# A diffusion-transformer layer on one core: attention's state scaling and query scaling in wide vector-engine operations, its output norm on the scalar engine, and a reordered gelu branch

## The chip, the cores and the metric

The kernel runs on one core of a Trainium2 chip. A core has a matrix engine (PE), a vector engine (DVE), a scalar engine (ACT), a general engine (POOL), and queues for DMA transfers, SP's among them. Each engine works through its own list of instructions in order, and waits where an instruction needs something that another engine or a transfer has not delivered. The metric is the device time of one execution in microseconds.

## The reference

One layer with 1024 latent tokens of width 1024 and 256 context tokens. What matters here, cut from the reference:

```
hl = modulate(rmsnorm(x, g_pre_mix), sh1, sc1)            # adaLN; sh1, sc1, gt1 ... from c @ w_ada
z_q, z_k, z_v, z_dec, z_og, z_f, z_rx, z_rg = split(hl @ w_in)
# group 1: bidirectional chunked gated linear attention, 4 heads, dk 64, dv 128
b    = cumsum(log_a);  q_t = q * exp(b);  k_t = k * exp(-b);  k_end = k * exp(b_last - b)
attn = where(tril, q_t @ k_t^T, 0)
o    = attn @ v + q_t @ s                  # s: the state before the chunk
s    = s * exp(b_last) + k_end^T @ v       # starts from the context's final state
y_gla = rmsnorm(o) * g_gla * silu(z_og)
# group 2: 2-D Fourier mixing of z_f.  group 3: centred conv + bidirectional RG-LRU scan h_rg
y_rg = h_rg * gelu(z_rg)
x = x + gt1 * rmsnorm(concat(y_gla, y_f, y_rg) @ w_out, g_post_mix)
x = x + gt2 * rmsnorm(swiglu(modulate(rmsnorm(x, g_pre_ffn), sh2, sc2)), g_post_ffn)
```

## The kernel before

Everything stays in fp32 precision: a product of large matrices is three PE passes (`mm3`, lines 84 to 86: high by high, high by low, low by high part). In names, `z` and `zn` are the banks of PSUM that take the input projection, transposed (`z`, 128x512) or not (`zn`, 128x256), `hl` is the modulated input, `w_hi` and `w_lo` are split weights. `z_v1` is a projection of values (a run of `zn`), `z_rg` the projection that gelu is applied to.

Attention takes two head pairs, p = 0 and 1, with two heads h and two directions d each, and goes over 8 blocks n of 128 tokens. Before the first block the states are made for all blocks (`gla_states`, which calls `gla_kv` for each direction and half q): PE transposes the keys (`k_tr`), multiplies them with the values (`kv`), DVE runs the recurrence (`tt`, line 532, one 128x128 step per block and direction), and ACT writes each state, multiplied by its chunk's exponential, into the state tile `St` (line 518, one 64x128 instruction for each head). The context's keys and states (`ctx_tr`, `ctx_st`) come ahead of that. In `gla_block` each block first forms `qx` = q times exp(c) (four 64x128 products, the two of d = 0 on DVE, those of d = 1 on POOL from the exchanged copy `qTs` of q), then `attn` (four matmuls), the masked `am` (DVE), and the output bank `o` (four matmuls, from `qx` with `St` and from `am` with the values). ACT squares and sums `o` (`jk`, line 587), POOL raises to the power of minus one half (`ors`), and DVE scales `o` into `on` (line 592).

The rest that the text names: `gate_ps` are banks of the RG-LRU gates, which ACT reads; `rg_scan` ends with `hR`, to which the second direction is added (line 648); `fourier` folds its input (`zo`, `zfold`) before the products `Z_ps`; `ada_row` (line 651) makes a row of the modulation: eight `ada_acc` steps of 128x1024 on DVE (line 658), then for each half a matmul that sums over partitions (`row_ps`, line 669) and a DVE step that writes `ada_row` (line 677). PSUM is two rings of four banks: `mm` (z, zn, o, and others) and `aux` (ctx_tr, k_tr, kv, attn, gate_ps, row_ps, Z_ps and others); a bank is free again when its last reader is done.

What order the instructions have on each engine is not written down: the kernel is built in a mode in which a scheduler decides it from the dependencies and its own estimates. Only table functions of ACT are chained in the order of the program. So an edit in one place can move instructions in many.

Of the kernel before, what the change touches and what calls it, by code (L numbers as in the profile page):

```python
# [16 lines left out]
P = 128  # L17
# [21 lines left out]
def tile_trunk(ctx: ExitStack, tc: tile.TileContext, A: dict):  # L39
# [26 lines left out]
    def aux(name="aux"):  # L66
        return psum.tile([P, 512], F32, tag="aux", bufs=4, name=name)
# [291 lines left out]
    def z_v1(blocks, c=False):  # L359
        z_N(w_v[1], 256, lambda ps, m: S.copy(vNc[1] if c else vN[1][m // 4][:, m % 4:m % 4 + 2, :], ps), blocks, c)  # L360
# [151 lines left out]
        return kn, last  # L512

    def gla_kv(p, d, q, kn, gs, tprev):
        def state(m, t):
            n = (7 - m) if d else m
            for h in range(2):
                S.mul(St[p][h ^ d][R[h], n, :], t[R[h]], gs[R[h], m:m + 1])  # L518

        if q == 0:  # L520
            state(0, s_ctx[p][d])
            tprev = s_ctx[p][d]
        kv = aux("kv")
# [12 lines left out]

    def gla_states(p):
# [25 lines left out]
    load(imask, A["imask"])  # L563
    on = [[None] * 2 for _ in range(2)]

    def gla_block(p, n):
        cs = slice(n * P, (n + 1) * P)
        qx, am = hp((P, 2, P), name="qx"), hp((P, 2, P), name="am")
        for d in range(2):
            for h in range(2):  # L570
                (G if d else V).tensor_mul(qx[R[h], h ^ d, :], (qTs if d else qT)[p][R[h], cs], Ex[p][d][R[h], cs])
# [237 lines left out]
    def fourier(zf, blk):  # L809
# [16 lines left out]
        jk = hp(name="fjk")[:, 0:256]
        V.tensor_mul(jk, f[:, 0, :], alt)
# [644 lines left out]
```

## Time and profile before

| | before |
|---|---|
| time, median of 3 runs | 1141.46 us (1141.27 to 1141.75) |
| time of the profiled execution | 1140.04 us |
| its span, first to last instruction | 1138.3 us |
| PE busy | 1082.4 us (95%) |
| DVE, ACT, POOL busy | 807.9 (71%), 506.8 (45%), 107.4 us (9%) |
| mean granted clock of PE | 0.975 |

The span is the length of the trace; the time of the same execution is 1.7 us more. PE is busy for all but 56 us of it. A clock of 1.0 is the full 2.4 GHz, 0.5 is 1.2 GHz; at the lower one the same matmul takes twice as long and PE counts as busy all the while, so a stretch at half clock costs time that no idle figure shows.

### The profile page before, as it was taken

The numbers are of one execution on the slowest core, as the hardware profiler recorded it, in microseconds if no ns is written. First come the engines' busy times: TensorE is split into PE (matmuls) and PEld (weight loads), VectorE is DVE, ScalarE is ACT, GpSimd is POOL, SyncE is SP. The second block draws the span as 40 slices with busy tenths as digits, with TensorE's granted clock in tenths as the row PEclk, the third lists the DMA queues.
The fourth block names the chain that finished last, engine by engine and source line by source line (L and its number), as shares of the span: only waits on it lengthen the run. The fifth ranks groups of instructions, "written<-read, shape, count | busy, mean of one in ns | idle before, by whom it ended". The sixth has DMA issues, their size and how long they took to land.

```text
span 1138.3 us, 15164 instructions
## 1 busy us (share of the span) xinstructions
PE 1082.4 (95%) x5547; PEld 903.2 (79%) x5547; DVE 807.9 (71%) x1386; ACT 506.8 (45%) x964; POOL 107.4 (9%) x133
## 2 busy tenths in 40 slices
PE   4899989989999999949999999999999999999997
PEld 2799887867789888837878888888888888888886
DVE  3474693648878366797879777777777568967684
ACT  3452768486273355654313333232323137654251
POOL 2310001213220011370000000000000000000100
PEclk8899999999999999978999999999999999999999
DMA  9802312112526222351273242324232468867571
GB/s 331 301 20 78 107 38 56 38 39 63 201 75 238 77 93 93 112 166 56 93 253 108 93 130 93 102 93 130 93 102 93 149 208 310 277 221 235 177 283 74
DMA packets 119970, 156.42 MB, mean 137 GB/s; under 512 B 8276, under 2 KB 70996, under 8 KB 119896
## 3 DMA queue, kind: packets, MB, share of 16 engines
q1 hardware_dynamic: 106536, 128.72, 34.7%
q10 hardware_dynamic: 13360, 26.75, 7.0%
q8 instruction: 43, 0.70, 0.2%
q14 instruction: 31, 0.25, 0.1%
HBM read 124.50 MB, written 28.57 MB: 134 GB/s over the span
## 4 chain that ended last, share of the span: by engine, by line
PE 81%; DVE 8%; ACT 4%; DMA 4%; issue 3%; POOL 0%; SPq 0%; DVEq 0%; POOLq 0%; ACTq 0%
PE prod L84 11%; PE prod L85 11%; PE prod L86 11%; PE dn L84 6%; PE dn L86 6%; PE dn L85 6%; PE z L84 3%; PE o_ps L86 3%; PE o_ps L84 3%; PE o_ps L85 3%; PE z L85 3%; PE z L86 3%; DMA wraw<-in_w_in 2%; ACT St L518 2%; PE zn L84 2%
## 5 line engine op out<-in xcount | busy, mean ns | idle before, releaser
L85 PE MATMUL dn<-dr,dl 128*128 128x512 f32 (+1 forms) x319 | 121.8, 382 | 0.0
L86 PE MATMUL dn<-dr,dl 128*128 128x512 f32 (+1 forms) x319 | 121.8, 382 | 0.0
L84 PE MATMUL dn<-dr,dl 128*128 128x512 f32 (+1 forms) x319 | 118.7, 382 | 0.0
L85 PE MATMUL zn<-w_lo,hl 128*128 128x256 f32 (+1 forms) x256 | 74.0, 290 | 0.0
L84 PE MATMUL zn<-w_hi,hl 128*128 128x256 f32 (+1 forms) x256 | 73.4, 289 | 0.2 <-ACT yfr L77 0.2
L86 PE MATMUL zn<-w_hi,hl 128*128 128x256 f32 (+1 forms) x256 | 73.0, 288 | 0.0
L84 PE MATMUL prod<-a,b_hi 128*128 128x512 f32 x176 | 69.6, 395 | 1.4 <-ACT b_hi L91 1.4
L86 PEld LDWEIGHTS dn<-dr,dl 128*128 128x128 f32 x319 | 60.0, 188 | 11.7
L85 PEld LDWEIGHTS dn<-dr,dl 128*128 128x128 f32 x319 | 60.0, 188 | 11.7
L85 PE MATMUL prod<-a,b_hi 128*128 128x512 f32 x176 | 69.2, 393 | 0.0
L84 PEld LDWEIGHTS dn<-dr,dl 128*128 128x128 f32 x319 | 60.0, 188 | 11.5
L84 PE MATMUL prod<-s,wb_hi 128*128 128x512 f32 x176 | 68.9, 391 | 0.0
L85 PE MATMUL prod<-s,wb_hi 128*128 128x512 f32 x176 | 68.5, 389 | 0.0
L86 PE MATMUL prod<-s,wb_lo 128*128 128x512 f32 x176 | 68.3, 389 | 0.0
L86 PE MATMUL prod<-a,b_lo 128*128 128x512 f32 x176 | 68.1, 391 | 0.0
L1110 ACT CAST b<-wf_raw 128x512 fp32r<-128x512 f32 x22 | 13.7, 622 | 115.0 <-PE prod L86 105.4
L84 PE MATMUL z<-hl,w_hi 128*128 128x512 f32 x160 | 64.8, 405 | 0.0
L85 PE MATMUL z<-hl,w_hi 128*128 128x512 f32 x160 | 63.7, 398 | 0.0
L86 PE MATMUL z<-hl,w_lo 128*128 128x512 f32 x160 | 63.4, 396 | 0.0
L1177 ACT CAST dl<-h 128x512 fp32r<-128x512 f32 x77 | 47.7, 620 | 35.0 <-issue 20.6
L1178 DVE TENSOR_TENSOR dl<-h,dl 128x512 fp32r<-128x512 f32 x77 | 52.6, 684 | 12.8 <-ACT dl L1177 12.8
L1234 POOL TENSOR_TENSOR rs<-s,mhalf 128x1 f32<-128x1 f32 x7 | 5.4, 774 | 553.3 <-DVE s L1233 553.3
(362 smaller groups left out, 2871.6 us busy)
## 6 DMA issues: line engine op xcount, KB each, us to landing
ada_raw<-in_w_ada SPq DMA_DIRECT2D x48, 512.0 KB, 6.3
h<-hd SPq DMA_DIRECT2D x77, 256.0 KB, 4.8
wd_raw<-in_w_down SPq DMA_DIRECT2D x77, 256.0 KB, 4.6
hd<-c ACTq DMA_DIRECT2D x55, 256.0 KB, 2.1
wf_raw<-in_w_gate SPq DMA_DIRECT2D x25, 512.0 KB, 4.1
wf_raw<-in_w_up SPq DMA_DIRECT2D x22, 512.0 KB, 4.7
wraw<-in_w_in SPq DMA_DIRECT2D x16, 512.0 KB, 4.2
xb<-in_x SPq DMA_DIRECT2D x8, 512.0 KB, 8.4
```

Of the source, the lines that this page charges most:

```text
L84: PE.matmul(out, lh, rh, start=start, stop=False)
L85: PE.matmul(out, lh, rl, start=False, stop=False)
L86: return PE.matmul(out, ll, rh, start=False, stop=stop)
L518: S.mul(St[p][h ^ d][R[h], n, :], t[R[h]], gs[R[h], m:m + 1])
L1110: S.copy(hi, u[:, 4:8])
L1177: S.copy(t[:, 0, :], raw)
L1178: V.tensor_sub(t[:, 1, :], raw, t[:, 0, :].bitcast(F32))
L1234: G.tensor_tensor(out=r, in0=s1, in1=mhalf, op=ALU.pow)
```

## The change

Five edits. States: the 64 ACT instructions that write `St` become wide DVE products, one for each head, direction and half (64x512 or 64x384), issued after all the `tt` of that half. Queries: `gla_q` forms q times exp(c) for four blocks at once with four 64x512 products on DVE, in place in `qT` and in the tile of exp(c), `la`; POOL has no part in it any more. Output norm: `on` moves from DVE to ACT. POOL's add for `hR` and three folds in `fourier` move to DVE. In the order of the program, all of `z_v1` now stands ahead of the context's states, and `z_rg(1)` right after `z_rg(0)`.

```
--- before.py
+++ after.py
@@ -512,14 +512,15 @@
         return kn, last
 
     def gla_kv(p, d, q, kn, gs, tprev):
-        def state(m, t):
-            n = (7 - m) if d else m
+        def states(m, w, t):
+
+            n = slice(8 - m - w, 8 - m) if d else slice(m, m + w)
             for h in range(2):
-                S.mul(St[p][h ^ d][R[h], n, :], t[R[h]], gs[R[h], m:m + 1])
+                V.tensor_mul(fl(St[p][h ^ d][R[h], n, :], d), t[R[h]], gs[R[h], m:m + w].unsqueeze(2).to_broadcast([64, w, P]))
 
         if q == 0:
-            state(0, s_ctx[p][d])
             tprev = s_ctx[p][d]
+            states(0, 1, tprev.unsqueeze(1))
         kv = aux("kv")
         for i, m in enumerate(order(q)):
             n = (7 - m) if d else m
@@ -530,8 +531,9 @@
         for i, m in enumerate(order(q)):
             tt = t4[:, i, :]
             V.scalar_tensor_tensor(tt, tprev, gs[:, m:m + 1], kv[:, i * P:(i + 1) * P], op0=ALU.mult, op1=ALU.add)
-            state(m + 1, tt)
             tprev = tt
+        w = len(order(q))
+        states(4 * q + 1, w, t4[:, 0:w, :])
         return tprev
 
     def gla_states(p):
@@ -563,23 +565,34 @@
     load(imask, A["imask"])
     on = [[None] * 2 for _ in range(2)]
 
+    qx = [None] * 2
+
+    def gla_q(p, h):
+
+        hs = slice(h * 512, (h + 1) * 512)
+        q, qs, e0, e1 = qT[p], qTs[p], Ex[p][0], Ex[p][1]
+        V.tensor_mul(q[R[0], hs], q[R[0], hs], e0[R[0], hs])
+        V.tensor_mul(e0[R[1], hs], q[R[1], hs], e0[R[1], hs])
+        V.tensor_mul(q[R[1], hs], qs[R[1], hs], e1[R[1], hs])
+        V.tensor_mul(e0[R[0], hs], qs[R[0], hs], e1[R[0], hs])
+        qx[p] = q, e0
+
     def gla_block(p, n):
         cs = slice(n * P, (n + 1) * P)
-        qx, am = hp((P, 2, P), name="qx"), hp((P, 2, P), name="am")
-        for d in range(2):
-            for h in range(2):
-                (G if d else V).tensor_mul(qx[R[h], h ^ d, :], (qTs if d else qT)[p][R[h], cs], Ex[p][d][R[h], cs])
+        if n % 4 == 0:
+            gla_q(p, n // 4)
+        am = hp((P, 2, P), name="am")
         at = [aux("attn")[:, 0:256].rearrange("p (d i) -> p d i", d=2) for _ in range(2)]
         for d in range(2):
             for h in range(2):
-                mark = PE.matmul(at[h][:, d, :], Kt[p][d][R[h], cs], qx[R[h], h ^ d, :], start=True, stop=True)
+                mark = PE.matmul(at[h][:, d, :], Kt[p][d][R[h], cs], qx[p][h ^ d][R[h], cs], start=True, stop=True)
         for h in range(2):
             V.tensor_mul(am[:, h, :], at[h][:, 0, :], wmask)
             V.copy_predicated(am[:, h, :], imask, at[1 - h][:, 1, :])
         o = mm("o")
         for h in range(2):
             oc = o[:, h * P:(h + 1) * P]
-            PE.matmul(oc, qx[:, h, :], St[p][h][:, n, :], start=True, stop=False)
+            PE.matmul(oc, qx[p][h][:, cs], St[p][h][:, n, :], start=True, stop=False)
             PE.matmul(oc, am[:, h, :], vN[p][n // 4][:, n % 4, h * P:(h + 1) * P], start=False, stop=True)
         ss = sm("oss", 2)
         jk = pool.tile([P, P], mybir.dt.bfloat16, tag="jk", bufs=1, name="jk")
@@ -589,7 +602,7 @@
         if n % 4 == 0:
             on[p][n // 4] = pg((P, 4, 256), name="on")
         for h in range(2):
-            V.tensor_scalar_mul(on[p][n // 4][:, n % 4, h * P:(h + 1) * P], o[:, h * P:(h + 1) * P], r[:, h:h + 1])
+            S.mul(on[p][n // 4][:, n % 4, h * P:(h + 1) * P], o[:, h * P:(h + 1) * P], r[:, h:h + 1])
         return mark
 
     def rg_gate(dst, u, blk, d, g, n):
@@ -645,7 +658,7 @@
         if d == 0:
             hR.append(a)
         else:
-            G.tensor_add(hR[blk], hR[blk], a)
+            V.tensor_add(hR[blk], hR[blk], a)
 
 
     def ada_row(c0, fn):
@@ -717,11 +730,10 @@
         vN[1][i] = pg((P, 4, 256), name="vN")
     w_q = [w_T(C_Q)]
     bs = [ctx_exp(p, d) for p, d in PD]
-    z_v1(range(4))
+    z_v1(range(8))
     kws = [ctx_tr(b) for b in bs]
     for (p, d), kw in zip(PD, kws):
         ctx_state(p, d, kw)
-    z_v1(range(4, 8))
     kt_begin(0)
     w_q.append(w_T(C_Q + P))
     def z_steps(w, h, ev):
@@ -814,14 +826,14 @@
         G.memset(o[:, 0:1], 0.0)
         rv = zf[:, 513:1024][:, ::-1]
         V.tensor_add(e[:, 1:512], zf[:, 1:512], rv)
-        G.tensor_sub(o[:, 1:512], zf[:, 1:512], rv)
+        V.tensor_sub(o[:, 1:512], zf[:, 1:512], rv)
         f = pg((P, 4, 256), name="zfold")
         er, orv = e[:, 257:513][:, ::-1], o[:, 257:512][:, ::-1]
         V.tensor_add(f[:, 0, :], e[:, 0:256], er)
         V.tensor_sub(f[:, 1, :], e[:, 0:256], er)
         G.memset(f[:, 2:4, 0:1], 0.0)
-        G.tensor_sub(f[:, 2, 1:], o[:, 1:256], orv)
-        G.tensor_add(f[:, 3, 1:], o[:, 1:256], orv)
+        V.tensor_sub(f[:, 2, 1:], o[:, 1:256], orv)
+        V.tensor_add(f[:, 3, 1:], o[:, 1:256], orv)
         cols = sm("fcol", 3)
         jk = hp(name="fjk")[:, 0:256]
         V.tensor_mul(jk, f[:, 0, :], alt)
@@ -865,11 +877,11 @@
         V.tensor_copy(yfr[2][:, blk, 0:1], cc[:, 0:1])
 
     z_rg(0)
+    z_rg(1)
     ada_step(9)
     w_og = [w_N([(C_OG, 256)])]
     for d in range(2):
         rg_scan(1, d, rg_gates(1, d))
-    z_rg(1)
     ada_step(0)
     alt = hp(name="alt")[:, 0:256]
     load(alt, A["alt"])
```

Where the scheduler put things. On DVE, at the states of p = 0 (names as above; `rgc` belongs to the context's RG-LRU), before:

```order
L532 SCALAR_TENSOR_TENSOR tt_1828<-tt_1828,gs_1753,kv_1819 128x128
L532 SCALAR_TENSOR_TENSOR tt_1848<-tt_1848,gs_1739,kv_1841 128x128
L532 SCALAR_TENSOR_TENSOR tt_1828<-tt_1828,gs_1753,kv_1819 128x128
L532 SCALAR_TENSOR_TENSOR tt_1848<-tt_1848,gs_1739,kv_1841 128x128
L532 SCALAR_TENSOR_TENSOR tt_1865<-tt_1828,gs_1753,kv_1858 128x128
L571 TENSOR_TENSOR qx_1991<-qT_1875,la_709 64x128 x2
L532 SCALAR_TENSOR_TENSOR tt_1865<-tt_1865,gs_1753,kv_1858 128x128 x2
L577 TENSOR_TENSOR am_1992<-attn_1997,cm_65 128x128
L571 TENSOR_TENSOR qx_2036<-qT_1875,la_709 64x128 x2
L578 COPY_PREDICATED am_1992<-imask_714,attn_1998 128x128
L577 TENSOR_TENSOR am_1992<-attn_1998,cm_65 128x128
L578 COPY_PREDICATED am_1992<-imask_714,attn_1997 128x128
```

and after the change, the end of the same piece of work:

```order
L575 TENSOR_TENSOR la_709<-qT_1855,la_709 64x512
L533 SCALAR_TENSOR_TENSOR tt_1849<-tt_1849,gs_1753,kv_1842 128x128
L590 TENSOR_TENSOR am_1975<-attn_1976,cm_65 128x128
L590 TENSOR_TENSOR am_2015<-attn_2016,cm_65 128x128
L574 TENSOR_TENSOR qT_1855<-qT_1855,la_709 64x512
L533 SCALAR_TENSOR_TENSOR tt_1849<-tt_1849,gs_1753,kv_1842 128x128
L576 TENSOR_TENSOR qT_1855<-qTs_1856,la_710 64x512
L591 COPY_PREDICATED am_1975<-imask_714,attn_1977 128x128
L590 TENSOR_TENSOR am_1975<-attn_1977,cm_65 128x128
L577 TENSOR_TENSOR la_709<-qTs_1856,la_710 64x512
L638 SCALAR_TENSOR_TENSOR rgc_1916<-rgc_1916,cx_507 128x512
L519 TENSOR_TENSOR St_1766<-tt_1849,gs_1753 64x3x128
```

In the kernel before nothing but `tt` and two `qx` stands ahead of the first `am`. After the change the last two `St` (one of them is the last row shown, its twin the next row), which `o` of block 0 reads because direction 1 ends at block 0, stand behind two `tt`, the second `gla_q`, four steps of `am` for blocks 0 and 1, and an `rgc`. In the whole piece, from the first `tt` to the last `St`, there are 14 `tt`, 8 wide `St` and the 4 products of the second `gla_q`.

On DVE again, at the rows of the modulation (`ada_row_2920` in the kernel before and `ada_row_2870` after are the row of g_post_mix, `ada_row_2958` and `ada_row_2908` that of g_pre_ffn), before:

```order
L807 TENSOR_TENSOR yfr_2864<-yfr_2864,a_2524 128x256
L807 TENSOR_TENSOR yfr_2865<-yfr_2865,a_2524 128x256
L658 SCALAR_TENSOR_TENSOR ada_acc_2931<-ada_raw_2934,s32_73,ada_acc_2931 128x1024
L658 SCALAR_TENSOR_TENSOR ada_acc_2931<-ada_raw_2937,s32_73,ada_acc_2931 128x1024
L658 SCALAR_TENSOR_TENSOR ada_acc_2931<-ada_raw_2940,s32_73,ada_acc_2931 128x1024
L658 SCALAR_TENSOR_TENSOR ada_acc_2931<-ada_raw_2943,s32_73,ada_acc_2931 128x1024
L658 SCALAR_TENSOR_TENSOR ada_acc_2931<-ada_raw_2946,s32_73,ada_acc_2931 128x1024
L658 SCALAR_TENSOR_TENSOR ada_acc_2931<-ada_raw_2949,s32_73,ada_acc_2931 128x1024
L658 SCALAR_TENSOR_TENSOR ada_acc_2931<-ada_raw_2952,s32_73,ada_acc_2931 128x1024
L658 SCALAR_TENSOR_TENSOR ada_acc_2931<-ada_raw_2955,s32_73,ada_acc_2931 128x1024
L677 SCALAR_TENSOR_TENSOR ada_row_2958<-row_ps_2959,g_row_2961 128x512
```

and after the change:

```order
L819 TENSOR_TENSOR yfr_2760<-yfr_2760,a_2452 128x256
L819 TENSOR_TENSOR yfr_2761<-yfr_2761,a_2452 128x256
L671 SCALAR_TENSOR_TENSOR ada_acc_2881<-ada_raw_2884,s32_73,ada_acc_2881 128x1024
L671 SCALAR_TENSOR_TENSOR ada_acc_2881<-ada_raw_2887,s32_73,ada_acc_2881 128x1024
L671 SCALAR_TENSOR_TENSOR ada_acc_2881<-ada_raw_2890,s32_73,ada_acc_2881 128x1024
L671 SCALAR_TENSOR_TENSOR ada_acc_2881<-ada_raw_2893,s32_73,ada_acc_2881 128x1024
L671 SCALAR_TENSOR_TENSOR ada_acc_2881<-ada_raw_2896,s32_73,ada_acc_2881 128x1024
L690 SCALAR_TENSOR_TENSOR ada_row_2870<-row_ps_2876,g_row_2878 128x512
L671 SCALAR_TENSOR_TENSOR ada_acc_2881<-ada_raw_2899,s32_73,ada_acc_2881 128x1024
L671 SCALAR_TENSOR_TENSOR ada_acc_2881<-ada_raw_2902,s32_73,ada_acc_2881 128x1024
L671 SCALAR_TENSOR_TENSOR ada_acc_2881<-ada_raw_2905,s32_73,ada_acc_2881 128x1024
L690 SCALAR_TENSOR_TENSOR ada_row_2908<-row_ps_2909,g_row_2911 128x512
```

Before, both halves of the first row were written ahead of the eight `ada_acc` of the second. Now the second half, from `row_ps_2876`, stands between the fifth and the sixth of them. On PE, where these banks are filled, the end of the last `z` of the gelu projection before:

```order
L86 MATMUL z_3059<-hl01_494,w_lo_2859 128x512
L84 MATMUL z_3059<-hl01_494,w_hi_2858 128x512
L85 MATMUL z_3059<-hl11_502,w_hi_2858 128x512
L86 MATMUL z_3059<-hl01_494,w_lo_2859 128x512
L669 MATMUL row_ps_2959<-ada_acc_2931,cm_65 128x512
L669 MATMUL row_ps_2964<-ada_acc_2931,cm_65 128x512
L600 MATMUL gate_ps_2990<-uT_707,gates_1905 128x512
L600 MATMUL gate_ps_2993<-uT_707,gates_1905 128x512
```

and after the change:

```order
L86 MATMUL z_2843<-hl01_494,w_lo_2755 128x512
L84 MATMUL z_2843<-hl01_494,w_hi_2754 128x512
L85 MATMUL z_2843<-hl11_502,w_hi_2754 128x512
L86 MATMUL z_2843<-hl01_494,w_lo_2755 128x512
L682 MATMUL row_ps_2876<-ada_acc_910,cm_65 128x512
L682 MATMUL row_ps_2909<-ada_acc_2881,cm_65 128x512
L682 MATMUL row_ps_2914<-ada_acc_2881,cm_65 128x512
L613 MATMUL gate_ps_2940<-uT_707,gates_1885 128x512
```

The matmul for `row_ps_2876` had its counterpart (`row_ps_2926`) 100 rows earlier, between matmuls of `o`. It now stands directly ahead of `row_ps_2909`, which needs the finished `ada_acc`.

## Rows read from the trace of the kernel before

**Rows 1.** Waits of PE: engine, line, waited for: total us, times, longest us.
```profile
PE o L582 <- ACT St L518: 4.4, 1, 4.4
...
PE ctx_tr L449 <- DVE b_c L443: 2.9, 2, 2.6
...
PE gate_ps L600 <- ACT qT L559: 2.0, 1, 2.0
PE Z_ps L837 <- DVE zfold L820: 1.9, 2, 1.7
...
PE row_ps L669 <- DVE ada_acc L658: 1.4, 2, 0.8
```

**Rows 2.** Windows: stretch, length, busy of PE, PEld, DVE, ACT, POOL, clock, DMA.
```profile
191.00:194.30 3.30, 1.34 (x12) 0.85 (x10) 1.56 (x6) 2.76 (x7) 0.00 (x0) 1.00 0.48 143
194.30:204.50 10.20, 10.20 (x40) 6.91 (x39) 4.88 (x19) 6.85 (x14) 0.94 (x2) 0.50 0.13 28
204.50:249.00 44.50, 44.50 (x281) 36.03 (x281) 26.55 (x79) 26.98 (x73) 13.87 (x22) 1.00 0.21 48
252.30:259.10 6.80, 4.95 (x16) 3.75 (x16) 2.60 (x7) 6.67 (x12) 0.00 (x0) 0.50 0.00 0
260.00:308.00 48.00, 48.00 (x246) 37.18 (x246) 42.00 (x88) 20.84 (x52) 18.21 (x21) 1.00 0.47 154
```

**Rows 3.** Timeline of ACT, 178 to 196 us: start, length, instructions.
```profile
184.50 8.24 ACT L518 ACTIVATE St<-tt,gs 64x128 f32<-64x128 f32 x20
192.76 0.60 ACT L559 ACTIVATE qT<-z 128x512 f32<-128x512 f32 x1
```

**Rows 4.** Timeline of DVE, 178 to 196 us.
```profile
180.18 0.35 DVE L532 SCALAR_TENSOR_TENSOR tt<-s_ctx,gs,kv 128x128 f32<-128x128 f32 x1 [6.99 <-PE kv L527]
```

**Rows 5.** Timeline of PE, 188 to 206 us.
```profile
189.35 1.46 PE L600 MATMUL gate_ps<-cx,gates 128*128 128x256 f32 x6
```

**Rows 6.** Timeline of ACT, 240 to 262 us.
```profile
242.48 11.53 ACT L518 ACTIVATE St<-tt,gs 64x128 f32<-64x128 f32 x28 [2.76 <-DVE tt L532]
```

**Rows 7.** Groups by line and form, 141 to 350 us: count | busy, mean ns.
```profile
L571 POOL TENSOR_TENSOR qx<-qTs,la 64x128 f32<-64x128 f32 x32 | 16.5, 516 | 121.3 <-DVE tt L532 112.6 <-DMA qTs<-qT 6.5 <-PE kv L527 0.7
...
L571 DVE TENSOR_TENSOR qx<-qT,la 64x128 f32<-64x128 f32 x32 | 9.9, 309 | 0.4
L592 DVE TENSOR_SCALAR on<-o,ors 128x128 f32<-128x128 f32 x32 | 9.7, 343 | 5.4 <-POOL ors L116 5.4
...
L587 ACT ACTIVATE jk<-o 128x128 bf16<-128x128 f32 x32 | 8.8, 274 | 23.6 <-PE o L583 15.3 <-DMA qTs<-qT 4.3 <-DVE am L577 1.6
...
L532 DVE SCALAR_TENSOR_TENSOR tt<-tt,gs,kv 128x128 f32<-128x128 f32 x24 | 7.2, 345 | 0.3
...
L494 DVE TENSOR_TENSOR Kt<-Kt,ek 128x512 f32<-128x512 f32 x4 | 2.7, 686 | 0.0
```

**Rows 8.** Timeline of DVE, 296 to 312 us.
```profile
298.63 10.52 DVE L658 SCALAR_TENSOR_TENSOR ada_acc<-ada_raw,s,ada_acc 128x1024 f32<-128x1024 f32 x8
310.38 0.69 DVE L677 SCALAR_TENSOR_TENSOR ada_row<-row_ps,g_row 128x512 f32<-128x512 f32 x1 [1.22 <-PE row_ps L669]
...
311.84 1.22 DVE L92 TENSOR_TENSOR w_lo<-wraw,w_hi 128x1024 fp32r<-128x1024 f32 x1
```

**Rows 9.** Timeline of PE, 305 to 313 us.
```profile
307.76 0.39 PE L85 MATMUL z<-hl,w_hi 128*128 128x512 f32 x1
307.99 0.39 PE L86 MATMUL z<-hl,w_lo 128*128 128x512 f32 x1
309.21 1.98 PE L669 MATMUL row_ps<-ada_acc,cm 128*128 128x512 f32 x4 [0.83 <-DVE ada_acc L658]
```

**Rows 10.** Timeline of POOL, 334 to 348 us.
```profile
335.52 3.26 POOL L648 TENSOR_TENSOR a<-a 128x1024 f32<-128x1024 f32 x1 [9.50 <-issue]
```

**Rows 11.** Timeline of DVE, 334 to 346 us.
```profile
335.36 1.22 DVE L92 TENSOR_TENSOR w_lo<-wraw,w_hi 128x1024 fp32r<-128x1024 f32 x1
338.82 3.29 DVE L807 TENSOR_TENSOR yfr<-yfr,a 128x256 f32<-128x256 f32 x3 [2.24 <-POOL a L648]
```

More of the change, by code (lines that the diff above doesn't have):

```diff
@@ L514, in gla_kv, with states @@
     def gla_kv(p, d, q, kn, gs, tprev):
-        def state(m, t):
-            n = (7 - m) if d else m
+        def states(m, w, t):
+            n = slice(8 - m - w, 8 - m) if d else slice(m, m + w)
             for h in range(2):
-                S.mul(St[p][h ^ d][R[h], n, :], t[R[h]], gs[R[h], m:m + 1])
+                V.tensor_mul(fl(St[p][h ^ d][R[h], n, :], d), t[R[h]], gs[R[h], m:m + w].unsqueeze(2).to_broadcast([64, w, P]))
         if q == 0:
-            state(0, s_ctx[p][d])
             tprev = s_ctx[p][d]
+            states(0, 1, tprev.unsqueeze(1))
         kv = aux("kv")
@@ L532, in gla_kv @@
             V.scalar_tensor_tensor(tt, tprev, gs[:, m:m + 1], kv[:, i * P:(i + 1) * P], op0=ALU.mult, op1=ALU.add)
-            state(m + 1, tt)
             tprev = tt
+        w = len(order(q))
+        states(4 * q + 1, w, t4[:, 0:w, :])
         return tprev
@@ L564, in tile_trunk, with gla_q @@
     on = [[None] * 2 for _ in range(2)]
+    qx = [None] * 2
+    def gla_q(p, h):
+        hs = slice(h * 512, (h + 1) * 512)
+        q, qs, e0, e1 = qT[p], qTs[p], Ex[p][0], Ex[p][1]
+        V.tensor_mul(q[R[0], hs], q[R[0], hs], e0[R[0], hs])
+        V.tensor_mul(e0[R[1], hs], q[R[1], hs], e0[R[1], hs])
+        V.tensor_mul(q[R[1], hs], qs[R[1], hs], e1[R[1], hs])
+        V.tensor_mul(e0[R[0], hs], qs[R[0], hs], e1[R[0], hs])
+        qx[p] = q, e0
     def gla_block(p, n):
         cs = slice(n * P, (n + 1) * P)
[L568 to L571, printed above, removed]
+        if n % 4 == 0:
+            gla_q(p, n // 4)
+        am = hp((P, 2, P), name="am")
         at = [aux("attn")[:, 0:256].rearrange("p (d i) -> p d i", d=2) for _ in range(2)]
@@ L574, in gla_block @@
             for h in range(2):
-                mark = PE.matmul(at[h][:, d, :], Kt[p][d][R[h], cs], qx[R[h], h ^ d, :], start=True, stop=True)
+                mark = PE.matmul(at[h][:, d, :], Kt[p][d][R[h], cs], qx[p][h ^ d][R[h], cs], start=True, stop=True)
         for h in range(2):
@@ L581, in gla_block @@
             oc = o[:, h * P:(h + 1) * P]
-            PE.matmul(oc, qx[:, h, :], St[p][h][:, n, :], start=True, stop=False)
+            PE.matmul(oc, qx[p][h][:, cs], St[p][h][:, n, :], start=True, stop=False)
             PE.matmul(oc, am[:, h, :], vN[p][n // 4][:, n % 4, h * P:(h + 1) * P], start=False, stop=True)
@@ L591, in gla_block @@
         for h in range(2):
-            V.tensor_scalar_mul(on[p][n // 4][:, n % 4, h * P:(h + 1) * P], o[:, h * P:(h + 1) * P], r[:, h:h + 1])
+            S.mul(on[p][n // 4][:, n % 4, h * P:(h + 1) * P], o[:, h * P:(h + 1) * P], r[:, h:h + 1])
         return mark
@@ L647, in rg_scan @@
         else:
-            G.tensor_add(hR[blk], hR[blk], a)
+            V.tensor_add(hR[blk], hR[blk], a)
     def ada_row(c0, fn):
@@ L719, in tile_trunk @@
     bs = [ctx_exp(p, d) for p, d in PD]
-    z_v1(range(4))
+    z_v1(range(8))
     kws = [ctx_tr(b) for b in bs]
@@ L723, in tile_trunk @@
         ctx_state(p, d, kw)
-    z_v1(range(4, 8))
     kt_begin(0)
@@ L816, in fourier @@
         V.tensor_add(e[:, 1:512], zf[:, 1:512], rv)
-        G.tensor_sub(o[:, 1:512], zf[:, 1:512], rv)
+        V.tensor_sub(o[:, 1:512], zf[:, 1:512], rv)
         f = pg((P, 4, 256), name="zfold")
@@ L822, in fourier @@
         G.memset(f[:, 2:4, 0:1], 0.0)
-        G.tensor_sub(f[:, 2, 1:], o[:, 1:256], orv)
-        G.tensor_add(f[:, 3, 1:], o[:, 1:256], orv)
+        V.tensor_sub(f[:, 2, 1:], o[:, 1:256], orv)
+        V.tensor_add(f[:, 3, 1:], o[:, 1:256], orv)
         cols = sm("fcol", 3)
@@ L867, in tile_trunk @@
     z_rg(0)
+    z_rg(1)
     ada_step(9)
@@ L871, in tile_trunk @@
         rg_scan(1, d, rg_gates(1, d))
-    z_rg(1)
     ada_step(0)
```

## Prediction

> **What bounds the kernel now.** I read the table of busy time first: PE works 1082.4 us of a span of 1138.3, so the kernel is bound by PE, and a change can pay only where PE idles (56 us in all) or runs at half clock. The list of PE's waits says where it idles. The longest stands at the entry of the feed-forward part, where the edits put nothing. The ones that the change can reach are `o` on ACT's `St` (4.4 us), `ctx_tr` on DVE (2.9), `gate_ps` on ACT's `qT` (2.0), `Z_ps` on DVE's `zfold` (1.9) and `row_ps` on `ada_acc` (1.4, of which 0.8 in this stage): 12.0 us by the list, taking 0.8 for the last [rows 1].
>
> Then the clock. After the wait of `gate_ps` PE ran at 0.50 from 194.3 to 204.5, busy all the while; 10.2 us of work at half clock is 5.1 us of loss [rows 2]. After the wait of `o` it ran at 0.50 from 252.3 to 259.1, 4.95 us busy, which is 2.5 us of loss [rows 2]. Between these places, 204.5 to 249 and 260 to 308, PE is busy every moment at a clock of 1.00 [rows 2]: work taken off DVE, ACT or POOL there gains nothing by itself.
>
> The timelines name the culprits. ACT wrote 20 `St` in a row for 8.24 us and only then made `qT` at 192.76, on which the gates' bank waited [rows 3]. Before the second head pair it wrote 28 in a row, 11.53 us, 0.41 each, and PE's `o` stood behind the last [rows 6]. So in the best case the change has about 12 + 5.1 + 2.5 = 19.6 us to win, and nothing else.
>
> **The change part by part.** I go by stages, each as what the old order lost less what the new order loses.
>
> *States and first blocks of p = 0 (141 to 205 us).* Old loss: 2.9 (`ctx_tr`), 2.0 (`gate_ps`) and 5.1 (half clock), together 10.0 [rows 1, 2]. The 61 `zn` that now stand ahead of `ctx_tr` are more than 7 us of PE work, so the first wait goes; with the 20 `St` off ACT, `qT` is early and the second goes too. What is late next is the last `St`, now on DVE. Before, the first `tt` stood at 180.18, released by `kv` [rows 4]. In the new order PE has 20 more `z` matmuls ahead of `kv` (0.23 us each, the spacing of two `z` in [rows 9], 4.6) and 2.9 less waiting, so the first `tt` comes at about 181.9. From there DVE must do 14 `tt` (0.345 as a single; overlapped about 0.3: 4.2), 8 wide `St` and 4 `gla_q`, and the steps of `am` and `rgc`. No row has a 64x512 product; the nearest is 128x512 at 0.686 [rows 7], which overlaps its neighbours to about 0.6. The lower bound is half of that by size if it went by partitions, which the 64x128 `qx` speaks against: 0.309 for a quarter of the columns [rows 7], so fixed cost and columns count. I take 0.60 for 512 columns and 0.46 for 384: 4 x 0.60 + 4 x 0.46 + 4 x 0.60 = 6.6 us. With 0.8 for `am` and 0.65 for `rgc`, 4.2 + 6.6 + 1.5 = 12.3 us, and the last `St` ends at about 194.2. PE has reached `o` of block 0 by 191.9 to 193.5 (its gates started at 189.35, now 2.9 earlier; 8 gates at 0.49, three took 1.46 [rows 5], and 10 `attn` at 0.16 to 0.32 take 5.5 to 7). So a new wait of 1 to 3 us, say 2.0, and since a wait of 2.0 us at this very place was followed by the half clock before, I charge its 5.1 again. New loss 7.1, gain **+2.9**; without the half clock +8.0.
>
> *States and blocks of p = 1 (205 to 308).* Old loss: 4.4 + 2.5 = 6.9 [rows 1, 2]. The 28 `St` leave ACT (11.53 us, [rows 6]); their wide form is 4.2 us on DVE, and the four `gla_q` products of each half another 2.4. On the new path: `k_tr` waits for the key scaling that `gla_q` now precedes on DVE (about 0.6, one such product), the gate banks 3 and 4 come free only when the last `tt` has read its `kv` bank (about 2.4), and ACT, which now scales 16 `on` here, reads `o` and copies `zf` later, so that PE waits for banks (2.5 by my count of ACT's order). An `on` on ACT lies between 0.274 (`jk`, which reads the same tile, [rows 7]) and 0.41 (`St`, same form of operation from another memory [rows 6]); I take 0.35, 5.6 us for 16, and DVE loses as many at 0.343 [rows 7]. 32 `on` together are 11.2 us on ACT, hidden by PE in p = 0, where ACT is busy 26.98 of 44.50 us [rows 2]; in p = 1 they are not all hidden. New loss 5.5, gain **+1.4**; with none of it +6.9, with a half clock of 2.5 behind one of these waits -1.1.
>
> The `qx` of POOL (32 at 0.516, 16.5 us) and DVE (32 at 0.309, 9.9 us) become 16 products of about 0.60 on DVE, 9.6 us [rows 7]: equal on DVE, and POOL is free. PE never waited for POOL's part, so this gains nothing alone.
>
> *The modulation's rows (308 to 312).* Before, DVE ran the 8 `ada_acc` without a break, 10.52 us, 1.3 each [rows 8], and PE, done with `z` at 308.4, waited 0.83 for the last [rows 9]. Now `row_ps_2876` is filled only when all `z` are done, and on DVE its `ada_row` stands ahead of three `ada_acc`; PE's next matmul needs the last of these. DVE cannot start the step earlier, and PE has nothing in between. The wait is one `ada_row`, 0.69 [rows 8], and three `ada_acc`, 3 x 1.3 = 3.9: 4.6 us in place of 0.83, so -3.8. A wait of 4.4 us before `o` was followed by a loss of 2.5 at half clock [rows 1, 2]; charged again, **-6.3**. This is the term I am surest of in sign, and it comes from the order alone.
>
> *Scan end and Fourier fold (312 to 346).* POOL's add took 3.26 us, its folds behind it [rows 10]; DVE's `yfr` stood idle 2.24 us for the add, and `Z_ps` waited 1.7 behind that [rows 11, 1]. On DVE the add is 128x1024, as the `w_lo` at 1.22 [rows 11]: 2.0 us less, and the folds shrink likewise. One table load less on ACT is hidden. Gain **+1.7**, at most the 1.9 of the wait; if DVE's extra 4 us came ahead of `zfold`, nothing.
>
> A rule bears on these moves: POOL's SBUF interfaces are shared with DVE, so an instruction of DVE with two SBUF inputs contends with POOL (the Trainium skill, "GPSIMD Engine Reference", section "Specifications"). By it DVE would also grow faster where POOL falls silent, at the 16.5 us of `qx`; half of these lie in p = 1, and if all 8 us came off DVE's path there, the gain of that stage would reach its upper bound, 6.9 in place of 1.4. But the same `w_lo` took 1.22 us beside POOL's add, at 335.36, and 1.22 with POOL idle, at 311.84 [rows 8, 11], and by that row the sum keeps the 1.4.
>
> *Sum.* 2.9 + 1.4 - 6.3 + 1.7 = -0.3 us, that is 1140.04 + 0.3 = 1140.3 for an execution like the profiled one; that one lies 1.4 below the median of 1141.46, so on the scale of the median 1141.8. Two small gains that I don't price, more `attn` pairs that overlap in p = 0 and an earlier weight split at the feed-forward entry, may give back somewhat under 1 us. I forecast **1141.0 us**, no change that can be told: 0.2%, 2.3 us, is what a measurement of this kernel tells from none. Its own range is 1139.2 to 1143.7, with a chance of 0.41.
>
> **The rivals.**
> *The clock holds (0.19).* Whether half clock follows a wait is not settled by its length: the 2.9 us before `ctx_tr` brought none, the 2.0 before `gate_ps` did, and 0.83 did not. If it stays at 1.00 after the new waits of p = 0 and of `row_ps`, then 8.0 + 1.4 - 3.8 + 1.7 = +7.3, 1134.2 us. For it: the new wait of p = 0 may be near 1 us. Against: gates and `attn` around it are the same thin work that ran at half clock.
> *ACT's new load is hidden and the row's wait is not followed by half clock (0.16).* 2.9 + 4.5 - 3.8 + 1.7 = +5.3, 1136.2. For it: DVE and ACT have 40% free in p = 0 [rows 2], and p = 1 differs by little.
> *ACT and DVE become the bound in p = 1 (0.24), slower.* A block of p = 1 on ACT now has two `jk`, two `on`, its share of gates and table loads; DVE was already at 42.00 of 48.00 us there [rows 2]. When either is later than PE by more than the ring of four banks holds, PE waits at `o` or at `z` in each later block. At 1.0 us for each of the last five blocks beyond what I charged, 5 us, and the sum is -5.3: 1146.8. It decides from about 0.5 us a block. Against it: the `on` that leave DVE give back 16 x 0.343 = 5.5 us there [rows 7].
>
> That gives faster 0.35, same 0.41, slower 0.24. The range must hold the first and third rivals' centres for 8 in 10: 1133.5 to 1147.5.
>
> **What would show it.** The waits of PE after the change: none at `ctx_tr` over 0.5 us and none on `qT`; `o` waiting on DVE's `St` by 1 to 3 us near 192; `row_ps` on `ada_acc` at 4.6 us (under 2 would break my largest term); no `Z_ps` wait over 0.5. The granted clock at 0.5 behind the first and the `row_ps` wait. A wide `St` at 0.6 to 0.7, an `on` on ACT at 0.27 to 0.41. Wrong I am likeliest by the clock, 2.5 to 5 us each time.

## Result and the profile after

The changed kernel took 1132.78 us (median of 4 runs, 1132.65 to 1134.18) beside 1141.37 us for the kernel before in the same runs: a ratio of 0.9933, 95% interval 0.9921 to 0.9946. It is 0.5 to 0.8% faster. I had forecast no change, 1141.0, with 0.35 for faster; the median lies 0.7 us under the low end of my range.

The profiled execution took 1134.18 us, span 1132.4, and is the slowest of its four, 1.4 us above their median; that of the kernel before was 1.3 us under its median. So the two traces differ by 5.9 us of span where the medians differ by 8.6, and 2.7 us of the result lie outside the pair of traces that can be compared row by row.

The waits of PE after the change (us in total, times, longest):

```profile
PE prod L84 <- ACT wa_hi L91: 9.7, 1, 9.7
PE row_ps L682 <- DVE ada_acc L671: 5.0, 2, 4.6
...
PE o L595 <- DVE St L519: 1.6, 1, 1.6
PE attn L588 <- DVE tt L533: 1.5, 1, 1.5
...
PE gate_ps L613 <- DVE tt L533: 1.1, 1, 1.1
PE z L84 <- ACT on L605: 1.0, 1, 1.0
...
PE o L596 <- DVE am L591: 0.8, 2, 0.4
PE attn L588 <- DVE am L590: 0.5, 1, 0.5
PE k_tr L509 <- PE k_tr L509: 0.4, 1, 0.4
PE fc_ps L853 <- DVE fcol L841: 0.4, 1, 0.4
PE o L595 <- ACT on L605: 0.2, 1, 0.2
```

Against [rows 1], `ctx_tr`, `o` on ACT's `St`, `gate_ps` on `qT` and `Z_ps` are gone. In their place stand `row_ps` with 4.6 us and ten waits of 0.2 to 1.6. (A second wait of `row_ps`, 0.4 us here, lies behind the output projection.) The windows (the clock is the seventh figure, after the five engines) show the rest:

```profile
194.40:201.20 6.80, 5.22 (x15) 4.42 (x16) 5.37 (x11) 5.43 (x8) 0.00 (x0) 0.50 0.00 0
201.60:240.00 38.40, 38.40 (x218) 30.60 (x216) 20.27 (x55) 18.23 (x57) 6.48 (x7) 1.00 0.23 55
240.00:302.00 62.00, 58.94 (x334) 44.09 (x333) 41.39 (x86) 33.80 (x84) 12.94 (x12) 1.00 0.37 120
307.40:310.80 3.40, 3.40 (x5) 1.24 (x4) 0.87 (x2) 0.00 (x0) 0.00 (x0) 0.55 0.00 0
```

Half clock still follows the first blocks, for 7 us in place of 10.2 [rows 2], and now follows `row_ps` for 3.4; the whole second head pair, where the kernel before lost 2.5 us to it, runs at 1.00. The row that my largest term spoke of reads on DVE and on PE:

```profile
302.32 0.69 DVE L690 SCALAR_TENSOR_TENSOR ada_row<-row_ps,g_row 128x512 f32<-128x512 f32 x1 [4.08 <-PE row_ps L682]
302.93 3.92 DVE L671 SCALAR_TENSOR_TENSOR ada_acc<-ada_raw,s,ada_acc 128x1024 f32<-128x1024 f32 x3
```

```profile
301.26 1.02 PE L682 MATMUL row_ps<-ada_acc,cm 128*128 128x512 f32 x2
306.90 3.68 PE L682 MATMUL row_ps<-ada_acc,cm 128*128 128x512 f32 x4 [4.62 <-DVE ada_acc L671]
```

DVE idles 4.08 us for the matmul, writes the row, runs the three `ada_acc` behind it, and PE stands still for 4.62: before it was 0.83 [rows 9]. The groups of the moved operations (count, busy us, mean ns):

```profile
L605 ACT ACTIVATE on<-o,ors 128x128 f32<-128x128 f32 x32 | 10.1, 369 | 15.1 <-POOL ors L116 13.0 <-POOL zo L826 2.0
...
L519 DVE TENSOR_TENSOR St<-tt,gs 64x512 f32<-64x512 f32 x8 | 5.5, 684 | 0.1
```

### The profile page after: what moved, and what is told of

Its sections match the earlier page's. It is cut to its first block, busy times and chain, and to the rows that moved or that the text cites. A ratio compares the mean times of both kernels' runs of the same rounds, so it can differ in the third digit from the quotient of the medians.

```text
span 1132.4 us, 15040 instructions
## 1 busy us (share of the span) xinstructions
PE 1078.5 (95%) x5547; PEld 900.1 (79%) x5547; DVE 810.4 (72%) x1370; ACT 490.2 (43%) x931; POOL 83.6 (7%) x93
## 4 chain that ended last, share of the span: by engine, by line
PE 83%; DVE 6%; DMA 4%; ACT 3%; issue 2%; POOL 1%; SPq 0%; DVEq 0%; POOLq 0%; ACTq 0%
PE prod L84 11%; PE prod L85 11%; PE prod L86 11%; PE dn L85 6%; PE dn L84 6%; PE dn L86 6%; PE z L84 3%; PE z L85 3%; PE z L86 3%; PE o_ps L85 3%; PE o_ps L86 3%; PE o_ps L84 3%; PE zn L85 3%; PE zn L86 3%; PE zn L84 2%; DMA wraw<-in_w_in 2%
## 5 line engine op out<-in xcount | busy, mean ns | idle before, releaser
L84 PEld LDWEIGHTS dn<-dr,dl 128*128 128x128 f32 x319 | 60.0, 188 | 11.7
L86 PEld LDWEIGHTS dn<-dr,dl 128*128 128x128 f32 x319 | 60.0, 188 | 11.7
L85 PE MATMUL o_ps<-wo_lo,yh 128*128 128x512 f32 x128 | 49.9, 392 | 0.0
```

Source lines behind the costliest of these rows:

```text
L84: PE.matmul(out, lh, rh, start=start, stop=False)
L85: PE.matmul(out, lh, rl, start=False, stop=False)
L86: return PE.matmul(out, ll, rh, start=False, stop=stop)
```

## The experiments

Times are medians of the timed runs, ratios are to the kernel before in the same runs. "By the output projection" compares where PE starts `o_ps` in the traces: 380.8 us before, 377.9 after the change. The part behind it, to the end of the span, took 757.4 us before and 754.4 after. PE's first `zn`, which stands ahead of every edit, starts at 60.6 us before and at 61.0 after, in the other runs between 59.9 and 62.1; this offset is called the start of the program, and it is named where it matters.

**One row of the modulation earlier.** In the changed kernel:

```
+    ada_step(1)
     z_rg(0)
     z_rg(1)
-    ada_step(9)
+    ada_step(8)
```

> The changed kernel with one edit: the last step of the g_post_mix row stands ahead of the two gelu projections in the program, so that both of its row_ps matmuls run early and DVE's eight ada_acc stand without a break. My theory (the wait of 4.62 us and 3.4 us of half clock behind it are a cost of the order alone): row_ps waits at most 1 us, no half clock near 307 us, and the time is 3.5 to 5.5 us under that of the changed kernel, about 1128. Rival (PE's slack is used up later anyway, by the scan and the fold that DVE and ACT must still finish): the wait moves to Z_ps or y_ps and the time stays within 1.5 us of 1132.8.

1129.87 us, 0.9897 (0.9884 to 0.9911). `row_ps` does not wait at this place any more (the 0.8 us left are at 585 us), there is no half clock near 307, and `o_ps` starts at 370.3, 7.6 us earlier than after the change. My theory holds in the place; the time is 2.9 us lower, less than the 3.5 I expected at least, because the entry of the feed-forward part took some back: PE waited 11.7 us for `wa_hi` there, not 9.7, and then did 4.8 us of work at half clock, not 3.2. In all that part took 757.6 us, 3.2 more than in the changed kernel. The rival's places, `Z_ps` and `y_ps`, show no wait.

**Second gelu product back behind the scan.**

```
     z_rg(0)
-    z_rg(1)
     ada_step(9)
...
+    z_rg(1)
     ada_step(0)
```

> The changed kernel with the second gelu projection put back behind the scan. My theory: the late row_ps goes as in the run before, worth 3.5 to 5.5 us, against one table load of 1.28 us and a later release of banks, of which PE sees at most 1 us: 1128 to 1131. Rival (both gelu products together are what removed the Z_ps wait): Z_ps or the zn behind it waits 1 to 2 us again and the row's gain is eaten, 1132 to 1134.

1130.0 us, 0.9899 (0.9885 to 0.9912). The row's wait goes (0.5), but `zn` now waits 2.5 us for ACT's `yfr` (the gelu itself, which reads `zn`'s bank), so the early place of the gelus is worth about that and costs the row's 7. `Z_ps` does not wait. PE waits 7.2 us at the feed-forward entry, not 9.7. The time is inside my theory's range, but its term for the banks, at most 1 us, is refuted by the 2.5 us at `zn`, which the rival had named.

**Output norm back on DVE.**

```
-            S.mul(on[p][n // 4][:, n % 4, h * P:(h + 1) * P], o[:, h * P:(h + 1) * P], r[:, h:h + 1])
+            V.tensor_scalar_mul(on[p][n // 4][:, n % 4, h * P:(h + 1) * P], o[:, h * P:(h + 1) * P], r[:, h:h + 1])
```

> The changed kernel with attention's output norm back on DVE. My theory: ACT was hidden but for the waits of z and o on ACT's on (1.0 and 0.2 us), DVE in the second head pair is as full as before, so that part is within 1 us; the order also puts row_ps early again, worth 3.5 to 5.5: 1127 to 1130. Rival (taking 11 us off DVE is what carries the gain of the second head pair): o or attn wait for DVE's am and on there, 2 to 6 us, and the time is 1131 to 1137.

1125.02 us, 0.9853 (0.9838 to 0.9868): 7.8 us under the changed kernel. The row is early here too, so the first experiment is its like, and against that one `o_ps` starts 2.4 us earlier, 0.5 of it from the start of the program: by these two programs `on` on ACT costs some 2 us in attention. The rival is refuted; the waits on `on` (1.0 and 0.2 us) are gone, and `o` and `attn` wait for DVE's `St` and `am` by at most 0.3 us more each. The time is below what I expected because `o_ps` starts 10.1 us earlier than in the changed kernel (0.8 of it from the start), where I had granted 3.5 to 5.5 for the row and nothing for `on`. The feed-forward part takes 1.6 us of it back (756.0 us against 754.4).

**Value projection back.**

```
-    z_v1(range(8))
+    z_v1(range(4))
     kws = [ctx_tr(b) for b in bs]
     for (p, d), kw in zip(PD, kws):
         ctx_state(p, d, kw)
+    z_v1(range(4, 8))
```

> The changed kernel with the second half of the value projection put back behind the context's states. My theory (the first term): ctx_tr waits again, 2 to 3 us, but PE then has those zn left as cover while DVE finishes the wide St, so part of the 3.5 us of waits at attn and o goes: 0 to 3 us slower, 1133 to 1136. Rival (the merge moves a wait and saves nothing): within 0.5 us of 1132.8, or faster.

1135.4 us, 0.9947 (0.9935 to 0.996), an interval that overlaps that of the changed kernel: not told apart. In the trace `ctx_tr` waits 2.6 us again, with 3.4 us at half clock behind it, but the waits on `tt` and `St` are gone in the first head pair and the clock is 1.00 from 194 to 202 us; `o_ps` starts 2.7 us earlier, 1.1 of it from the start of the program. All of it is lost again in the feed-forward part (11.4 us of wait at its entry, 757.4 us in all). The time is inside my theory's range, but the reason isn't the one I gave: the merge won nothing that can be seen, and in this program it is what brings the waits and the half clock of the first head pair.

**States back on ACT** (`gla_kv` as before, the rest as changed).

```
-                V.tensor_mul(fl(St[p][h ^ d][R[h], n, :], d), t[R[h]], gs[R[h], m:m + w].unsqueeze(2).to_broadcast([64, w, P]))
+                S.mul(St[p][h ^ d][R[h], n, :], t[R[h]], gs[R[h], m:m + 1])
```

> The changed kernel with the scaled states back on ACT, 64 instructions of 64x128. My theory (the long runs of St on ACT were the loss that the change wins back): PE waits for ACT's St before o of both head pairs, 4 us or more each time with half clock behind, and DVE's list at the entry of the feed-forward part stands as in the kernel before, worth 2 us more: 1139 to 1145. Rival (the wide queries, which take POOL's part out of the path, carry the gain): under 1136.

1145.84 us, 1.0055 (1.0038 to 1.0071), 13 us above the changed kernel, slower than before, and 0.8 beyond my range. `o_ps` starts 7.9 us later than in the changed kernel, though the program started 0.6 earlier, and the part behind it takes 3.4 more. PE waits for ACT at both head pairs, but at the first one it is the gates that wait, not `o`:

```profile
PE prod L84 <- ACT wa_hi L91: 11.2, 1, 11.2
PE o L593 <- ACT St L518: 6.5, 1, 6.5
PE row_ps L680 <- DVE ada_acc L669: 5.1, 2, 4.6
...
PE gate_ps L611 <- ACT qT L559: 2.6, 1, 2.6
PE gate_ps L611 <- ACT rgc L77: 2.3, 1, 2.3
```

**POOL's adds back on POOL.**

```
-            V.tensor_add(hR[blk], hR[blk], a)
+            G.tensor_add(hR[blk], hR[blk], a)
... and G for the three folds of zo
```

> The changed kernel with the hR add and the three folds back on POOL. My theory: Z_ps waits 1.5 to 2 us again behind POOL's 3.3 us add, nothing else moves: 1134 to 1135.5. Rival (it was the gelu products' place that freed Z_ps): within 0.6 us of 1132.8.

1136.6 us, 0.9967 (0.9956 to 0.9978). `Z_ps` waits 1.9 us again, 1.6 the longest, where [rows 1] has 1.9 and 1.7. The move is worth 1.9 us by the spans of the traces (2.7 when the start of the program, 0.8 earlier here, is taken out) and 3.8 by the medians, more than I said; the place is right.

**States alone** in the kernel before.

> The kernel before with one edit, the wide states on DVE. My theory: both waits on ACT and both half-clock stretches (2.0 + 5.1, 4.4 + 2.5) go or shrink, a new wait of 1 to 2 us on DVE's St comes, row_ps stays early and the feed-forward entry as before: 8 to 11 us under 1141.3, 1130 to 1133, about all that the whole change won. Rival (St needs the other edits, since DVE with qx, on and St together becomes late): under 4 us won, 1137.5 or more.

1129.33 us beside 1140.59, 0.9908 (0.9892 to 0.9924): 11.3 us won, 0.3 beyond my range. That is at least as much as the whole change won, 8.6; the two intervals just touch. The new wait on DVE's `St` that I expected did not come: no `St` and no `qT` stands among PE's waits:

```profile
PE prod L84 <- ACT wa_hi L91: 11.9, 1, 11.9
PE ctx_tr L449 <- DVE b_c L443: 2.9, 2, 2.6
PE x_tr L1032 <- DVE xn L1024: 2.7, 1, 2.7
PE Z_ps L839 <- DVE zfold L822: 1.9, 2, 1.6
...
PE row_ps L671 <- DVE ada_acc L660: 1.2, 2, 0.8
PE attn L577 <- POOL qx L573: 0.8, 1, 0.8
```

and the clock is 1.00 through the blocks of both head pairs:

```profile
163.40:166.70 3.30, 3.30 (x16) 3.30 (x17) 3.30 (x17) 1.53 (x4) 0.00 (x0) 0.50 0.12 25
185.00:240.00 55.00, 54.74 (x357) 44.46 (x354) 40.27 (x117) 27.02 (x69) 18.22 (x32) 1.00 0.25 58
240.00:302.00 62.00, 59.78 (x287) 44.36 (x286) 53.72 (x114) 28.95 (x60) 21.79 (x22) 1.00 0.37 122
```

The first line is a stretch that the kernel before does not have: 3.4 us at half clock behind the wait of `ctx_tr`, 1.7 us of loss.

**Norm and value projection both back.** The two diffs above together.

> The changed kernel with two edits undone: the output norm on DVE, and the second half of the value projection behind the context's states. By the lists of the engines row_ps is early, and at the feed-forward entry DVE's last wf_raw stands ahead of three more of the differences s than in the run with the norm alone put back. My theory: 1125.0 less 1.5 to 3 us for that entry (its wait on wa_hi falls from 8.8 to about 7.2 us), and ctx_tr's wait of 2.6 us is paid back by shorter waits for St: 1121 to 1124. Rival (ctx_tr's wait is a loss in full, and the entry's gain is made up by half clock elsewhere): 1125 to 1127.

1124.0 us, 0.9859 (0.9842 to 0.9877). Inside my theory's range, at its edge: the entry's wait fell to 6.6 us and the part from `o_ps` on to 752.7 us from 756.0, while `o_ps` starts 0.7 us later than with the norm alone put back. Against the norm alone back (1125.02) the intervals overlap, so neither is shown to be the better; both beat both kernels.

**Queries alone** in the kernel before (`gla_q` and its uses).

> The kernel before with one edit, q times exp(c) in wide products on DVE. My theory (PE never waited for POOL's part, so the wide form alone wins nothing; ACT's St still end last): PE's waits on ACT stay at 2 and 4.4 us, 1139 to 1142.5. Rival (four blocks at once free DVE and POOL on the path of attn): more than 3 us won, under 1137.5.

1137.39 us beside 1140.36, 0.9984 (0.9971 to 0.9998): faster, but by no more than 0.3%. The median lies 1.6 us under my range and just inside the rival's. The waits on ACT stand at 4.3 and 1.5 us, as my theory said, so the 3 us of the medians do not come from there; what they come from is open, because the trace is that of one of the two long executions (1144.35 us, see the last section) and no short one was kept.

**Output norm alone** on ACT.

> The kernel before with one edit, the output norm on ACT. Its list on DVE at the feed-forward entry has the last wf_raw ahead of three more differences s. My theory: that entry's wait falls from 11.6 to about 7 us with less half clock, 4 to 6 us won, and on itself costs 1 to 3 us in attention, where ACT is behind its St: 1136.5 to 1139.5. Rival (moving on off DVE helps attention itself): PE's waits in attention get shorter and the time is under 1135.

1140.63 us, 1.0002 (0.999 to 1.0014). No gain, where I expected 2 to 5 us. The entry's wait fell to 6.2 us as its order said, and the part from `o_ps` on took 4.1 us less; but `o_ps` started 3.8 us later. In the second head pair `attn` waits 4.3 us for ACT's `tr` (a step of the RG-LRU gates) and `o` another 1.2 for `St`, in place of the 4.4 for `St` before, and `z` and `o` wait 2.1 in all for `on`. My theory took the cost of `on`, 1 to 3 us, too small here.

**Value projection alone** early.

> The kernel before with one edit, the whole value projection ahead of the context's states. My theory: ctx_tr's wait of 2.9 us goes, but ACT's 20 St still stand ahead of qT, so the gates wait longer by about as much: within 1.5 us of the kernel before, 1139.5 to 1142. Rival (the wait is simply removed): 2.5 to 3.5 us won, about 1138.

1139.35 us, 0.999 (0.9978 to 1.0002). No difference that can be told, as I expected, but not by the way that I gave: `ctx_tr` does not wait, and `gate_ps` waits no longer for `qT` than before, 1.7 us. What took the gain back are two waits of `attn` for `qx`, 1.1 us, and the clock: half of full speed for 17.1 us from 189.0, 15.1 of them PE work, in place of 10.2, which is 2.4 us more loss.

**States, queries and POOL's adds.** Three edits in the kernel before.

> Three of the five edits: wide states, wide queries, POOL's adds on DVE; the norm stays on DVE, the value projection and the second gelu product stay where they were. By the lists row_ps is early and the feed-forward entry has the shorter order. My theory: no long wait but ctx_tr's 2.9 and Z_ps below 0.5, the gelu's later place costs 1 to 2.5 us at zn, 1122 to 1125. Rival (the second gelu product's early place is needed): over 1126.

1127.4 us, 0.989 (0.9872 to 0.9909). Above my range. `ctx_tr` waits 2.9 us, `zn` 2.5 for `yfr`, the upper end of what I granted, and `o` of the second head pair 1.1 for `St`; the program started 1.4 us later than with the states alone. The rival is right that the second gelu's early place is worth something, 2.5 us, once the row is not late. Together the edits beat the states alone by no more than their intervals.

## Why the forecast missed

*States of p = 0, forecast +2.9: right in sum, in part by luck.* The waits around `attn` and `o` are 1.5, 0.5, 1.6 and 0.4 at `k_tr`, 4.0 us in all, twice the 2.0 that I charged; half clock covers 5.2 us of PE work, a loss of 2.6, half of the 5.1 that I charged. New loss 6.6, where I had 7.1; gain 3.4. The last `St` ended at 195.8, not 194.2. A wide `St` took 684 ns, as its neighbour in [rows 7]; the 0.60 that I took for overlap did not come.

*p = 1, forecast +1.4: too low, the second of the two steps that failed.* I charged 5.5 us of new waits; they are 1.1, 1.0, 0.8 and 0.2, 3.1 us. The gain is 6.9 - 3.1 = 3.8. I had ACT's bank waits at 2.5 where they were 1.2, the gate banks at 2.4 where they were 1.1, and 0.6 at `k_tr` where there is none. An `on` on ACT took 369 ns against my 350.

*The row, forecast -6.3: right.* 4.62 - 0.83 = 3.8, and half of 3.4 us, 1.7: -5.5 by the trace; the first experiment gave 7.6 back by the output projection, 0.4 of it the start. The wait came from the lists of the engines alone; the half clock was 0.8 us dearer in the forecast.

*Fourier fold, forecast +1.7: about right.* From the gates behind the row to `o_ps` PE took 67.6 us against 69.8 before, +2.2.

*The step that failed most* is "two small gains that I don't price", one of them "an earlier weight split at the feed-forward entry", under 1 us together. From `o_ps` to the end the changed kernel is 3.0 us shorter. It had no edit there. PE waits 9.7 us in place of 11.6 and then does 3.2 us of work at half clock in place of 4.9; the wait and the two stretches before:

```profile
PE prod L84 <- ACT wa_hi L91: 11.6, 1, 11.6
```

```profile
513.60:518.50 4.90, 4.90 (x12) 3.85 (x13) 4.83 (x7) 1.41 (x2) 0.00 (x0) 0.50 0.00 0
```

and after:

```profile
508.60:511.80 3.20, 3.20 (x8) 2.52 (x9) 2.87 (x3) 1.99 (x4) 2.91 (x2) 0.50 0.00 0
```

ACT's `wa_hi` is made from DVE's last `wf_raw` (a difference of weights), and the scheduler put that at one of three places on DVE's list, in this stretch of it behind six, three or two `s` (sums and differences of the layer's input blocks; `c` is a sum with a finished product, `b` the low part of a weight):

```
c s s b s s wf_raw s s wf_raw   before; row earlier; value proj. back; states back; states alone; queries alone; value proj. alone
s b c s wf_raw s wf_raw s s s   changed kernel; norm back; POOL's adds back
s b wf_raw c s wf_raw s s       gelu back; norm + value proj. back; norm alone; states + queries + POOL
```

The wait of `prod` for `wa_hi` is 10.6 to 11.9 us in the seven of the first order, 8.8 to 9.7 in the three of the second, 6.2 to 7.2 in the four of the third, without an overlap. The part from `o_ps` to the end falls into the same three groups: 756.4 to 757.8 us, 754.4 to 756.0, 752.7 to 754.0. ACT's `wa_hi` in the trace of before, released by that `wf_raw`, and in the one with the gelu back, where it did not wait:

```profile
512.49 1.04 ACT L91 CAST wa_hi<-wf_raw 128x1024 fp32r<-128x1024 f32 x1 [2.87 <-DVE wf_raw L1115]
```

```profile
501.33 1.04 ACT L91 CAST wa_hi<-wf_raw 128x1024 fp32r<-128x1024 f32 x1
```

I did not move this order by itself, so that it sets the wait is argued from fourteen programs and their traces, not shown by an edit. The sum by the traces is then 3.4 + 3.8 - 5.5 + 2.2 + 3.0 = 6.9, less 0.4 by which this execution was already late at the first `zn`, 6.5 against the 5.9 measured; 0.6 is not accounted for. To this come the 2.7 us of the pair of executions against the medians. Of the 7.2 us between the forecast of -0.3 and this sum, 3.0 are the entry and 2.4 the second head pair.

*The row on which I set DVE's contention with POOL aside* showed one side only. The `w_lo` of 1.22 us at 335.36 stood beside an add that took POOL 3.26 us [rows 10, 11]. At POOL's other add of that form the same trace has the reverse:

```profile
289.19 2.86 DVE L92 TENSOR_TENSOR w_lo<-wraw,w_hi 128x1024 fp32r<-128x1024 f32 x1
```

```profile
288.58 2.39 POOL L648 TENSOR_TENSOR a<-a 128x1024 f32<-128x1024 f32 x1 [2.53 <-issue]
```

So at both meetings the one that began second was the slower: POOL's add by 0.9 us at 335.52, DVE's `w_lo` by 1.6 us at 289.19. I had read DVE's row at the meeting where POOL paid. How much of the second head pair's gain comes from POOL's silence is open.

*The rivals.* "The clock holds" lies nearest in time, 1134.2, but not by its mechanism: the clock fell at both places. "ACT and DVE become the bound in p = 1" is refuted: PE's waits there are 3.1 us in all, less than I had charged without it. The main reason for the gain is in none of them: the states alone give 11.3 us, near what I priced for the ACT runs (2.0 + 5.1 + 4.4 + 2.5 = 14), and what took part of it back are the late row (2.9 us by the times) and `on` on ACT (2 us by the traces). My theory for the states was that a new wait and half clock on DVE eat 7 us of it. With the value projection merged they do (6.6 us); without the merge, alone or with the other edits, DVE has its `St` done in time in the first head pair and the clock stays at 1.00 in its blocks.

## What to carry to other kernels

When a scheduler lays out the engines' lists, compare the lists through to the end of the program and price every place where the bound engine waits behind a moved instruction: two such places, where no edit changed an instruction, differed by 7 us (to the output projection) and by 2 to 4 us here, as much as the edits. Test a change of several parts part by part: the states alone won at least as much as all five, and the changed kernel became faster when the norm, or the second gelu projection, was put back. Here a long run of small instructions on an engine whose next work was waited for paid when it became a few wide ones on another engine; moving the norm's small ones onto the relieved engine cost some 2 us of that.

## What was not expected of the hardware

The same wait was followed by very different stretches at half clock. With the queries alone, PE waited 4.3 us for `o`, as the kernel before did (4.4), and then ran at half clock for 20.5 us, busy nearly all of it, where before it was 6.8 [rows 2]:

```profile
252.40:272.90 20.50, 20.35 (x67) 15.32 (x68) 9.82 (x21) 10.24 (x20) 2.22 (x2) 0.50 0.00 0
```

That execution took 1144.35 us; ten of the twelve of this kernel lay between 1136.95 and 1138.5 and one more at 1143.93. The mean granted clock was 0.972 in the two long ones and 0.978 to 0.981 in the ten, so the clock goes with these 7 us of spread; the trace of no short one is there to compare. The wait of `ctx_tr`, 2.6 and 0.3 us, shows it in little: ahead of it the states alone have no edit, and they ran at half clock for 3.4 us behind it (the line at 163.40 above), where the kernel before did not:

```profile
161.40:175.00 13.60, 13.27 (x113) 11.80 (x113) 11.75 (x38) 8.42 (x15) 0.00 (x0) 1.00 0.27 78
```

What decided it is open.

DVE's wide `St` did slow down beside POOL. With the states alone, where POOL still formed `qx`, a 64x512 `St` took 769 ns in the mean; in the changed kernel, without POOL's `qx`, 684. Within the first of these traces the four that no `qx` overlaps took 0.68 to 0.69 us each, the four beside `qx` 0.75 to 0.95; a pair of either kind, with POOL's rows:

```profile
239.37 1.82 DVE L519 TENSOR_TENSOR St<-tt,gs 64x512 f32<-64x512 f32 x2
241.22 1.38 DVE L533 SCALAR_TENSOR_TENSOR tt<-tt,gs,kv 128x128 f32<-128x128 f32 x5
242.52 1.38 DVE L519 TENSOR_TENSOR St<-tt,gs 64x512 f32<-64x512 f32 x2
```

```profile
237.73 2.91 POOL L573 TENSOR_TENSOR qx<-qTs,la 64x128 f32<-64x128 f32 x5
```

The rule on shared interfaces that I weighed (an instruction of DVE with two SBUF inputs contends with POOL; the Trainium skill, "GPSIMD Engine Reference", section "Specifications") agrees with these rows. The same shows at the feed-forward entry of the kernel before, where a `wf_raw` of 128x512 took 1.24 us at 509.42, beside POOL's `s`, and 0.68 at 511.78, behind it.
